# Runs of small TensorE instructions in the planned order of a two-layer decoder trunk

## The chip, the core and the metric

The kernel runs on one core of a Trainium2 chip. A core has five engines that work at the same time, each through its own queue in order: TensorE (matrix products; PE in the profile, its weight loads PEld), VectorE (DVE), ScalarE (ACT), GpSimd (POOL) and SyncE (SP, which here issues all DMA transfers). An engine waits at an instruction until its semaphores say that the inputs are there. The metric is the time of one execution in device microseconds (us). It is the median of several runs.

## The reference, cut to what matters

The program computes a trunk of two layers over 256 tokens of width 1024, in float32. Each layer is one attention part and one feed-forward part, both between normalisations:

```python
for l in range(DEPTH):                                   # 2
    h = _rms_norm(x, g_pre_mix[l])
    parts = jnp.split(h @ w_in[l], split_at, axis=-1)    # 1024 x 2840: q, six k/v sets, gates, fox q/k/v, forget
    o_nsa = _nsa_mixer(...)     # 8 heads, 2 kv groups: compressed + selected + window attention, gated
    o_fox = _fox_mixer(...)     # 8 heads of causal attention with a forget bias
    mix = jnp.concatenate([o_nsa, o_fox], axis=-1) @ w_out[l]
    x = x + _rms_norm(mix, g_post_mix[l])
    h = _rms_norm(x, g_pre_mlp[l])
    y = jnp.square(jax.nn.relu(h @ w_up[l])) @ w_down[l]  # 1024 x 4096, 4096 x 1024
    x = x + _rms_norm(y, g_post_mlp[l])
return x
```

At this length all four key blocks are among the selected ones, so the selected branch is plain causal attention, and so is the window branch.

## The kernel before, in words

**The work.** Tokens stand in two halves of 128. A weight matrix arrives in pieces of up to 512 KB (`wraw`). ScalarE rounds each piece to a high part `whi`, VectorE subtracts to get the low part `wlo`, and TensorE takes three rounded products instead of one exact one (`mm3`, line 683): activation high by weight high, activation high by weight low, activation low by weight high. These *weight products* are 2,592 of TensorE's instructions, most of them 512 columns wide.

**The other instructions.** TensorE has 609 more products, which read no `whi` or `wlo`. The text calls them small. In the attention part of each layer they are:

- transposes in full float32 against the identity in `cst`, whose output goes to a PSUM tile `s`: probabilities `pr` in threes (`probs_T`, line 1279), keys, q and others in fours. The text calls these T.
- scores of the NSA heads, `s<-kx,qS` and `x<-kx,qS` (`nsa_scores`, line 1234): rounded and 128 by 128, like the weight products.
- fox scores `s<-fkT,fqT` (`fox_scores`, line 1223): groups that use 64 rows of the array. The text calls them K.
- products of probabilities with values, `o<-prT,vS` and the like (`pv`, line 1298): groups that use 64 columns. The text calls them V.
- products in 32 columns for the compression network (`o<-w,kstk`), and rounded transposes against `identr`.

**The order.** Nobody writes the order of instructions by hand. The program first records every operation with its inputs (`Recorder.add`, line 206), a sequence number (`key`) and an estimated cost (`_cost`, line 466). Then `Recorder.schedule` (line 316) plays the five engines through time. Whenever an engine is free, it takes the ready operation with the lowest rank whose tiles fit in the buffers that are free. For TensorE the rank is the key; for the other engines it is a due time, which `deadlines` (line 260) works back from TensorE's planned times. `order` (line 288) repeats this for five passes and two starting ranks and for each of five stages (bounds in `stages`), and keeps the ranks whose planned end was earliest. `emit` (line 417) writes the operations out in that order; line 424 issues every one of them, so almost every row of the profile has L424. A `stretch` is a group of products that the planner keeps together as one operation: the three transposes of one `pr`, one group of fox scores, one group of values.

In its plan the planner charges TensorE 90 ns when it goes from the full array to a group in part of it and 200 ns when it leaves such a group for any other shape (`ENTER`, `LEAVE`, line 44). It charges nothing between weight products and full-array transposes.

**Buffers.** PSUM has eight banks: three for tag `s`, two each for `x` and `acc`, one for `o` (`psum`, line 550). Raw weights have nine buffers, `whi` and `wlo` seven each (line 50). SyncE issues DMAs in the planned order, each when its buffer is free.

**The start.** The first 512 columns of the input projection come in eight transfers (`first`), then weight pieces, x (four transfers) and constants alternate on SyncE's queue. While TensorE multiplies the second chunk (288 columns wide, in four pieces of 12 products each), ScalarE takes the squares of x (`squares_of_x`, line 709; rows `rl<-x`) and VectorE the factor `rsqrt`, which the two small products of `row_scales` (line 1169) spread over the columns.

Of the kernel before, what the change touches and what calls it, by code (L numbers as in the profile page):

```python
# [45 lines left out]
EVKEY = 1  # L46
FIRSTS = [(k, k + 1) for k in range(8)]
NFIRST = 768
UPK = 7
TOK, WBUFS, RBUFS = 6, 7, 9  # L50
LOAD_LEAD, SPLIT_LEAD = 12, 1
# [125 lines left out]


class Op:
    __slots__ = ("engine", "name", "args", "kw", "key", "urgent", "cost", "deps", "succs", "bufs",  # L180
                 "missing", "ready", "start", "end", "tile", "rank")


class Recorder:
# [21 lines left out]
    def add(self, engine, name, args, kw):  # L206
        if self.group is not None:
            assert engine == "tensor"
            self.group.append((name, args, kw))
            return  # L210
        op = Op()
        op.engine, op.name, op.args, op.kw = engine, name, args, kw
        op.key = len(self.ops) if self.key is None else self.key
        if self.lane is not None and self.key is None:
            op.key = self.lane + LANE * (len(self.ops) - self.lane)
        op.urgent = self.hot
        views = []
        for _, a, k in args[2] if name == "stretch" else [(name, args, kw)]:
            views += [(i == 0, v) for i, v in enumerate(a) if isinstance(v, View)]
            views += [(i in ("out", "accum_out"), v) for i, v in k.items() if isinstance(v, View)]  # L220
        op.tile = _tile(op) if engine == "tensor" else None
        op.cost = _cost(op, views) + SLACK.get(engine, 0)
        deps = {} if self.after is None else {self.after: -1e9}
        op.bufs = []
        for is_out, v in sorted(views, key=lambda x: x[0]):
            b, m = v.buf, v.mask()
            if b not in op.bufs:
                op.bufs.append(b)

            def against(entries):  # L230
                for o, p, q, bank in entries:
                    if o is not op and o not in deps and (
                            (bank and engine == "tensor") or
                            (p[0] < v.p[1] and v.p[0] < p[1] and (m & q).any())):
                        deps[o] = _latency(o, op)

            against(b.writes)
            entry = (op, v.p, m, is_out and b.psum and engine == "tensor")
            if is_out:
                against(b.reads)  # L240
                b.writes = [w for w in b.writes if not (
                    w[0] in deps and v.p[0] <= w[1][0] and w[1][1] <= v.p[1] and not (w[2] & ~m).any())]
                b.writes.append(entry)
            else:
                if b.psum:
                    for o, _, _, _ in b.reads:
                        if o.engine != engine and o is not op and o not in deps:
                            deps[o] = 130.0
                b.reads.append(entry)
        op.deps = deps  # L250
        for b in op.bufs:
            if not b.ops:
                self.fifo.setdefault(b.tag, []).append(b)
            b.ops += 1
        op.succs = []
        for d in deps:
            d.succs.append(op)
        self.ops.append(op)
# [57 lines left out]
    def schedule(self):  # L316
# [35 lines left out]
                    taken[b.tag] = n + 1  # L352
            return True

        force = False
        events = [(0.0, 0, None)]
        count, out, live = 0, [], set()
        while events:
            t, _, released = heapq.heappop(events)
            if released is not None:  # L360
                free[released] += 1
            if events and events[0][0] == t:
                continue
            for e, ops in waiting.items():
                while busy[e] <= t:
                    best = None
                    for op in ops:
                        if op.ready <= t and (best is None or (best.urgent, -best.rank) < (op.urgent, -op.rank)) and fits(op):
                            best = op
                    if best is None:  # L370
                        break
                    if not best.urgent and e != "tensor" and not force:
                        q = hot[e]
                        while q and q[0].start is not None:
                            q.popleft()
                        memo = {}
                        if any(estimate(op, memo) < t + WAIT * best.cost for op in list(q)[:4] if op.start is None and fits(op)):
                            break
                    ops.remove(best)
                    for b in best.bufs:  # L380
                        if b not in live:
                            live.add(b)
                            free[b.tag] -= 1
                            head[b.tag] += 1
                    best.start = t
                    out.append(best)
                    if e == "sync":
                        busy[e] = t + 450
                        bus = max(bus, t + 1150) + best.cost + RAMP.get(loads, 0)
                        best.end = bus + 900 + (LATE if loads >= len(FIRSTS) else 0)  # L390
                        loads += 1
                    else:
                        busy[e] = best.end = t + best.cost
                        if e == "tensor" and best.tile != tiled:
                            busy[e] = best.end = best.end + (tiled == (P, P)) * ENTER + (tiled != (P, P)) * LEAVE
                            tiled = best.tile
                    count += 1
                    heapq.heappush(events, (busy[e], count, None))
                    for b in best.bufs:
                        left[b] -= 1  # L400
                        if not left[b]:
                            count += 1
                            heapq.heappush(events, (best.end + (260 if b.psum else 150), count, b.tag))
                    for s in best.succs:
                        s.ready = max(s.ready, t, best.end + s.deps[best])
                        s.missing -= 1
                        if not s.missing:
                            waiting[s.engine].append(s)
                            count += 1
                            heapq.heappush(events, (s.ready, count, None))  # L410
            force = not events and len(out) < len(self.ops)
            if force:
                heapq.heappush(events, (t + 100, 0, None))
# [22 lines left out]
def _tile(op):  # L436

    up = lambda n: next(m for m in (32, 64, P) if n <= m)
    lhsT = op.args[1]
    return (P, P) if op.name == "transpose" else (up(lhsT.shape[0]), up(int(np.prod(lhsT.shape[1:]))))  # L440
# [25 lines left out]
def _cost(op, views):  # L466

    out = op.args[0] if op.args else op.kw["out"]
    n = int(np.prod(out.shape[1:]))
    part = 100 * (out.shape[0] < P)  # L470
    if op.engine == "gpsimd":
        return 200 + 0.72 * n + 10 * int(np.prod(out.shape[1:-1]))
    if op.engine == "sync":
        v = views[0][1]
        return v.shape[0] * int(np.prod(v.shape[1:])) * 4 / 360.0
    if op.engine == "tensor":
        if op.name == "stretch":
            side = P // min(op.tile)
            return sum(_product(*x[:2], side) for x in op.args[2][::side])
        return _product(op.name, op.args, 1)  # L480
    if op.engine == "vector":
        if op.name == "reciprocal":
            return 60 + 6.5 * n
        if op.name == "tensor_reduce":
            n = int(np.prod(op.args[1].shape[1:]))
        fast = op.name in ("tensor_copy", "tensor_scalar", "memset") and not any(v.buf.psum for _, v in views)
        aps = sum(isinstance(v, View) for v in op.args[2:4]) if op.name == "tensor_scalar" else int(
            op.name == "scalar_tensor_tensor" and isinstance(op.args[2], View))
        return 68 + part + 64 * aps + n * (0.52 if fast else 1.04) + 10 * (op.name == "tensor_tensor_reduce")
    src = op.args[1]  # L490
    aps = sum(isinstance(op.kw.get(k), View) for k in ("bias", "scale", "accum_out"))
    return n / 1.2 + (55 if src.buf.psum else 92) + 93 * aps
# [1139 lines left out]
```

## Time and profile before

| | before |
|---|---|
| time, median of 3 runs | 620.45 us (620.43 to 620.82) |
| the profiled execution | 620.69 us, of which the span is 618.4 us |
| TensorE busy | 611.2 us, 99% of the span |
| its weight loads | 511.7 us, 83% |
| VectorE, ScalarE busy | 467.0 us (76%), 391.6 us (63%) |
| chain that ended last | TensorE 99% |

A row of a group says: line, engine, operation, output<-inputs, shape, count, busy us, mean ns of one, and the idle time before it. In a row of the timeline the first number is the start in us and the second the length from there to the end of the last instruction merged into it. Products overlap, each beginning while the one before still runs, so the price of a product is read from start to start of neighbouring rows and not from its length.

The layers show as stretches: attention of the first layer to about 125 us, its feed-forward part to about 310 us, attention of the second layer to about 430 us, its feed-forward part to the end.

### The profile page before, as it was taken

To read this page: it belongs to the slowest core of one execution; us is meant where nothing else is said; L and a number is where in the kernel's file an instruction comes from. 1 tells how busy PE (TensorE), PEld (TensorE's weight loads), DVE (VectorE), ACT (ScalarE), POOL (GpSimd) and SP (SyncE) were. 2 spreads that over 40 slices of the span, in tenths; PEclk is the share of its full clock that TensorE was granted. 3 is DMA by queue.
4 is the path that set the end of the run, shared out by engine and by line. 5 is a ranking of instruction groups with operands and counts; after the bars stand their busy time and mean duration, and the time that the engine had idled before them with its cause. 6 is when DMAs were issued, how large, how long until landed. Compare 5 with 4: busy or idle time off the path is not lost.

```text
span 618.4 us, 9735 instructions
## 1 busy us (share of the span) xinstructions
PE 611.2 (99%) x3430; PEld 511.7 (83%) x3430; DVE 467.0 (76%) x1029; ACT 391.6 (63%) x768; POOL 9.2 (1%) x20
## 2 busy tenths in 40 slices
PE   9999999999999999999999999999999999999995
PEld 7988887788888888888888888777888888888884
DVE  7799998789966567556598899896996575566544
ACT  6767978567655556555466768775776456556522
POOL 0000100000000000000000021000000000000000
PEclk9999999999999999999999999999999999999999
DMA  8987547518755565554346782553386555555001
GB/s 321 400 323 259 204 143 256 181 40 316 239 196 190 180 203 194 190 193 138 109 153 228 256 306 83 202 206 103 131 284 218 187 201 174 201 194 183 33 1 68
DMA packets 34817, 118.86 MB, mean 192 GB/s; under 512 B 4144, under 2 KB 4304, under 8 KB 34768
## 3 DMA queue, kind: packets, MB, share of 16 engines
q1 hardware_dynamic: 34768, 118.23, 55.8%
q8 instruction: 27, 0.44, 0.3%
q14 instruction: 22, 0.18, 0.1%
HBM read 117.15 MB, written 1.07 MB: 191 GB/s over the span
## 4 chain that ended last, share of the span: by engine, by line
PE 99%; DVE 0%; DVEq 0%; issue 0%; ACT 0%
PE s L424 35%; PE acc L424 31%; PE x L424 25%; PE o L424 7%; DVE x L424 0%; DVE m L424 0%; DVEq L1628 0%; DVE rsqrt L424 0%; ACT rl L424 0%
## 5 line engine op out<-in xcount | busy, mean ns | idle before, releaser
L424 DVE TENSOR_TENSOR wlo<-wraw,whi 128x1024 fp32r<-128x1024 f32 (+1 forms) x188 | 225.2, 1200 | 98.0 <-ACT whi L424 58.1
L424 ACT ACTIVATE whi<-wraw 128x1024 fp32r<-128x1024 f32 (+1 forms) x188 | 195.0, 1041 | 100.9 <-PE acc L424 68.5
L424 PE MATMUL s<-xT,whi 128*128 128x512 f32 x448 | 106.5, 390 | 0.0
L424 PEld LDWEIGHTS s<-xT,whi 128*128 128x128 f32 x448 | 83.3, 188 | 16.8
L424 PE MATMUL x<-whi,aT 128*128 128x512 f32 x256 | 88.6, 390 | 0.0
L424 PE MATMUL acc<-whi,aT 128*128 128x512 f32 x256 | 88.3, 389 | 0.0
L424 PEld LDWEIGHTS s<-xT,wlo 128*128 128x128 f32 x448 | 57.4, 191 | 2.2
L424 PE MATMUL s<-xT,wlo 128*128 128x256 f32 x448 | 58.1, 283 | 0.0
L424 PEld LDWEIGHTS acc<-whi,aT 128*128 128x128 f32 x256 | 48.0, 188 | 10.0
L424 PEld LDWEIGHTS x<-whi,aT 128*128 128x128 f32 x256 | 48.1, 188 | 9.5
L424 PE MATMUL x<-wlo,aT 128*128 128x512 f32 x128 | 50.0, 390 | 0.0
L424 PE MATMUL acc<-wlo,aT 128*128 128x512 f32 x128 | 49.9, 390 | 0.0
L424 ACT ACTIVATE pr<-pr,st 128x256 f32<-128x256 f32 (+1 forms) x96 | 42.8, 449 | 7.2 <-DVE st L424 6.7
L424 PE MATMUL acc<-whi,xT 128*128 128x512 f32 (+1 forms) x128 | 37.4, 354 | 0.0
L424 PE MATMUL acc<-xT,whi 128*128 128x512 f32 x128 | 36.1, 402 | 0.0
L424 PE MATMUL x<-whi,xT 128*128 128x512 f32 x112 | 35.8, 399 | 0.0
L424 ACT ACTIVATE h<-s 128x256 f32<-128x256 f32 x56 | 21.2, 378 | 16.0 <-PE s L424 16.0
L424 ACT ACTIVATE rl<-h 128x512 f32<-128x512 f32 x28 | 17.7, 633 | 18.1 <-DVE h L424 18.1
L424 PEld LDWEIGHTS acc<-wlo,aT 128*128 128x128 f32 x128 | 24.0, 188 | 5.0
L424 ACT ACTIVATE rl<-x 128x512 f32<-128x512 f32 x24 | 14.6, 610 | 21.0 <-PE x L424 16.9
L424 PEld LDWEIGHTS x<-wlo,aT 128*128 128x128 f32 x128 | 24.1, 188 | 4.5
L424 PEld LDWEIGHTS acc<-xT,whi 128*128 128x128 f32 x128 | 22.7, 188 | 5.3 <-ACT whi L424 0.8
(218 smaller groups left out, 966.0 us busy)
## 6 DMA issues: line engine op xcount, KB each, us to landing
wraw<-in_w_up_dram SPq DMA_DIRECT2D x64, 512.0 KB, 4.0
wraw<-in_w_down_dram SPq DMA_DIRECT2D x64, 512.0 KB, 4.2
wraw<-in_w_in_dram SPq DMA_DIRECT2D x36, 512.0 KB, 4.3
wraw<-in_w_out_dram SPq DMA_DIRECT2D x16, 512.0 KB, 6.7
w<-in_cmp_w_k_dram SPq DMA_DIRECT2D x8, 512.0 KB, 5.4
w<-in_cmp_w_v_dram SPq DMA_DIRECT2D x8, 512.0 KB, 5.6
bias<-sums SPq DMA_DIRECT2D x8, 384.0 KB, 6.9
first<-in_first_dram SPq DMA_DIRECT2D x7, 384.0 KB, 6.2
```

Source lines behind the costliest of these rows:

```text
L424: getattr(getattr(self.nc, op.engine), name)(*[real(v) for v in args], **{k: real(v) for k, v in kw.items()})
```

## The change

`schedule` now knows which of TensorE's operations are small: those that read no `whi` or `wlo` tile. Two rules act at the moment when TensorE is free and the lowest-ranked ready operation has been found. Neither acts on operations marked urgent.

- If that operation is small, the last one taken was not, and it has been ready for less than `HOLD` = 300 ns, the planner counts the small operations that are ready and fit. If there are fewer than two, it takes the lowest-ranked weight product instead, if one is ready.
- If the last one taken was small and the best is a weight product, the planner takes a small one instead, when one is ready whose rank is at most `REACH` = 40 above the weight product's.

```diff
+HOLD = 300
+REACH = 40
...
+        op.small = engine == "tensor" and not any(v.buf.name.startswith(("whi", "wlo")) for _, v in views)
...
-        force = False
+        force = small_last = False
...
                     if best is None:
                         break
+                    if e == "tensor" and best.small and not small_last and not best.urgent and t < best.ready + HOLD:
+                        more = [op for op in ops if op.ready <= t and fits(op)]
+                        if sum(op.small for op in more) < 2:
+                            best = min((op for op in more if not op.small), key=lambda op: op.rank, default=best)
+                    if e == "tensor" and small_last and not best.urgent and not best.small:
+                        more = [op for op in ops if op.small and op.ready <= t and op.rank < best.rank + REACH and fits(op)]
+                        best = min(more, key=lambda op: op.rank, default=best)
...
                         busy[e] = best.end = t + best.cost
+                        small_last = best.small if e == "tensor" else small_last
```

The number of instructions stays the same on every engine. In TensorE's order the unbroken runs of small instructions go from 135 to 82; the shortest that vanish are single NSA score products that stood between weight products. How the kinds follow one another in TensorE's order, counted in the two programs (T, K and V as above; R is any rounded full-array product, weight products and NSA scores alike):

| kind followed by kind | before | after |
|---|---|---|
| V by R, V by T | 6, 2 | 2, 6 |
| K by R, K by T, K by V | 4, 3, 1 | 4, 2, 2 |
| R by V, T by V | 6, 1 | 5, 1 |
| R by K, T by K | 8, 0 | 6, 2 |
| blocks of T entered | 82 | 78 |

Because the due times of the other engines are worked back from TensorE's plan, their orders change too. At the start SyncE's order after `first` goes from wraw, wraw, x, wraw, x, wraw, x, x, wraw, cst to wraw, x, x, wraw, x, x, cst, wraw, wraw, wraw, and ScalarE takes the first squares of x right after the split of the first piece, where it first took two splits.

More of the change, by code (lines that the diff above doesn't have):

```diff
@@ L179 @@
 class Op:
-    __slots__ = ("engine", "name", "args", "kw", "key", "urgent", "cost", "deps", "succs", "bufs",
+    __slots__ = ("small", "engine", "name", "args", "kw", "key", "urgent", "cost", "deps", "succs", "bufs",
                  "missing", "ready", "start", "end", "tile", "rank")
```

## The prediction

> **What bounds the kernel now.** I read the page first, then the busy time by stretch, then what TensorE's loads wait for, then the timeline.
>
> ```profile
> span 618.4 us, 9735 instructions
> PE 611.2 (99%) x3430; PEld 511.7 (83%) x3430; DVE 467.0 (76%) x1029; ACT 391.6 (63%) x768; POOL 9.2 (1%) x20
> PEclk9999999999999999999999999999999999999999
> PE 99%; DVE 0%; DVEq 0%; issue 0%; ACT 0%
> ```
>
> TensorE is busy for 611.2 of 618.4 us at full granted clock, and 99% of the chain that ended last lies on it. A busy PE could still hide waits, so the stretches and the waits come next: attention of the first layer (60 to 125 us), a feed-forward stretch, and the loads' waits in the first of these.
>
> ```profile
> 60.00:125.00 65.00, 65.00 (x420) 51.67 (x419) 57.81 (x210) 49.37 (x146) 3.39 (x8) 1.00 0.58 198
> 160.00:300.00 140.00, 140.00 (x709) 119.64 (x708) 90.24 (x109) 77.61 (x104) 0.00 (x0) 1.00 0.57 187
> ```
>
> ```profile
> PEld s L424 <- ACT pr L424: 0.9, 3, 0.3
> PEld s L424 <- DVE pr L424: 0.4, 1, 0.4
> PEld s L424 <- ACT prT L424: 0.4, 1, 0.4
> ```
>
> The second and third numbers of a stretch are its length and PE's busy time: no gap in either. Loads waited for an input 5 times in this stretch, 1.7 us together, and a load runs ahead of its product, so the products lost less than that. The change can therefore take only what switching between kinds of products costs, and it can add waits that are not there now.
>
> **What a switch costs.** Prices are read from start to start.
>
> ```profile
> 99.25 0.39 PE L424 MATMUL acc<-wlo,oT 128*128 128x512 f32 x1
> 99.48 0.40 PE L424 MATMUL acc<-whi,oT 128*128 128x512 f32 x1
> 99.72 0.49 PE L424 MATMUL s<-cst,pr 128*128 128x128 f32 x3
> 99.96 0.48 PE L424 MATMUL acc<-whi,oT 128*128 128x512 f32 x1
> 100.37 0.93 PE L424 MATMUL s<-fkT,fqT 64*128 64x128 f32 x8
> 101.23 0.51 PE L424 MATMUL acc<-wlo,oT 128*128 128x512 f32 x1
> 101.66 0.87 PE L424 MATMUL o<-prT,vS 128*64 128x256 f32 x8
> ...
> 104.42 0.87 PE L424 MATMUL s<-cst,pr 128*128 128x128 f32 x6
> 105.05 0.48 PE L424 MATMUL acc<-whi,oT 128*128 128x512 f32 x1
> 105.36 0.40 PE L424 MATMUL x<-whi,oT 128*128 128x512 f32 x1
> 105.59 0.40 PE L424 MATMUL x<-wlo,oT 128*128 128x512 f32 x1
> ```
>
> A weight product after another takes 0.23 (99.25 to 99.48). Three T take 0.24 (99.72 to 99.96) and make the next product 0.08 longer (105.05 to 105.36 is 0.31): 0.32 for three, 0.107 each. That is what a T costs anyway, since six T in one run take 0.63 + 0.08 = 0.71 after a V, which itself makes the first one longer. So joining two runs of T saves 0.00 to 0.02.
>
> K costs 0.10 on entry (99.96 to 100.37 is 0.41, against 0.31 for a product after T) and 0.11 on exit to a product. After K and before V one product takes 0.43 (101.23 to 101.66): 0.23, that 0.11, and 0.09 for the entry to V. An exit from V to T costs 0.71 less six T at 0.109, 0.055.
>
> ```profile
> 412.62 0.93 PE L424 MATMUL s<-fkT,fqT 64*128 64x128 f32 x8
> 413.47 1.52 PE L424 MATMUL o<-prT,fV 128*64 128x256 f32 x16
> 414.92 0.50 PE L424 MATMUL acc<-whi,oT 128*128 128x512 f32 x1
> 415.26 0.40 PE L424 MATMUL acc<-wlo,oT 128*128 128x512 f32 x1
> ```
>
> Here K goes straight to V. K takes 0.85, as it did at 100.37 (0.86), and V to R costs 0.34 - 0.23 = 0.11. So K next to V pays neither exit nor entry, 0.20 less than with a product between.
>
> The Trainium skill ("TensorEngine Tiling (Array Packing)", Key Properties) says that changing the tiling mode drains TensorE. The 0.09 to 0.11 above agree. By that rule alone changes of mode would be what counts, and the table of the change has 31 for K and V before and 30 after: one less, 0.1 to 0.2 us. The 0.055 for an exit to T is beyond it.
>
> ```profile
> 91.94 0.39 PE L424 MATMUL s<-kx,qS 128*128 128x256 f32 x2
> 92.17 0.63 PE L424 MATMUL x<-kx,qS 128*128 128x512 f32 x2
> 92.63 0.40 PE L424 MATMUL x<-whi,oT 128*128 128x512 f32 x1
> 92.87 0.39 PE L424 MATMUL x<-wlo,oT 128*128 128x512 f32 x1
> ```
>
> NSA scores cost 0.23 for two of 256 columns, 0.23 for one of 512, and 0.24 for the weight product behind them: they are as cheap among weight products as these among themselves. More than half of the 53 vanished runs are scores of this kind alone, and their vanishing is worth nothing in these rows.
>
> **The sum.** (1) Exits from V: before 6 x 0.11 + 2 x 0.055 = 0.77, after 2 x 0.11 + 6 x 0.055 = 0.55, so -0.22. (2) Exits from K: 4 x 0.11 + 3 x 0.055 = 0.605, after 4 x 0.11 + 2 x 0.055 = 0.55, so -0.055. (3) Entries to V from outside K or T: 6 to 5, -0.09. Entries to K from T (none before, two after) are unseen; between 0 and the 0.10 from a product I take 0.10, since V after T pays too, and 0 would give 0.2 more. (4) Blocks of T: 82 to 78 at 0.00 to 0.02, -0.05. Together -0.4.
>
> (5) Weight products near small ones are a little longer. The numbers below are the shortest, the median and the longest.
>
> ```profile
> L424 PE MATMUL x<-whi,oT x64: 387/396/484, 92.6 to 428.0; 128*128 128x512 f32 x64
> L424 PE MATMUL x<-whi,aT x256: 389/389/481, 148.3 to 606.2; 128*128 128x512 f32 x128
> ```
>
> The median is 7 ns above that of the feed-forward stretch. Over some 300 products (my estimate: two or three behind each of the 135 runs) this is 2 us. If it belongs to the runs, 40% fewer of them give back 0.8; if it belongs to the stretch, nothing. I take 0.3, nearer to nothing, because more than half of the vanished runs are such scores.
>
> (6) Waits. I cost them at nothing, and name the cover. A small instruction held back costs none while a weight product is ready, and in this stretch TensorE has no gap. One pulled forward is taken only when the plan has it ready. What would be late next is the copying of a finished `s` bank:
>
> ```profile
> L424 ACT ACTIVATE prT<-s 128x384 f32<-128x384 f32 x32 | 15.0, 483 | 3.2 <-PE s L424 3.1
> ```
>
> 0.48 us for a bank that three T fill in 0.33. With three banks the third group of a run is covered, a fourth is not. Bounds: the 1.7 us above and, supposed, as much in the second layer could vanish from the loads (at most -3, since some of it is hidden), or every mixed run could wait (below). I keep 0.
>
> (7) The start, where the orders of SyncE and ScalarE change. The third weight piece of the second chunk moves behind x and the constants.
>
> ```profile
> 7.80 0.33 SPq L424 DMA_DIRECT2D wraw<-in_w_in_dram  x1
> ...
> 12.41 0.33 SPq L424 DMA_DIRECT2D wraw<-in_w_in_dram  x1
> ```
>
> ```profile
> wraw<-in_w_in_dram SPq DMA_DIRECT2D x8, 288.0 KB, 5.0
> ```
>
> ```profile
> 16.44 0.42 PE L424 MATMUL acc<-whi,xT 128*128 128x288 f32 x2
> ...
> 22.13 0.39 PE L424 MATMUL s<-cst,rsqrt 128*128 128x128 f32 x2
> ```
>
> ```profile
> 14.66 0.69 ACT L424 ACTIVATE whi<-wraw 128x576 fp32r<-128x576 f32 x1
> ```
>
> ```profile
> 15.38 0.76 DVE L424 TENSOR_TENSOR wlo<-wraw,whi 128x576 fp32r<-128x576 f32 x1 [0.22 <-ACT whi L424]
> ```
>
> It goes out at 12.41 at the latest (before at 7.80) and lands 5.0 later, by 17.4. The chunk's products run 0.132 apart (43 from 16.44 to 22.13), so the third piece is wanted at 16.44 + 24 x 0.132 = 19.6. The split on ScalarE takes about 0.7, the subtraction 0.76: ready near 19.0 even if both start at the landing. It is hidden with 0.6 to spare; without that cover it costs what it is late, up to 0.5.
>
> Sum: -0.4 - 0.3 = -0.7 us. Against the profiled execution of 620.69 (span 618.4 and 2.3 around it) that is 620.0; the median of the runs is 0.24 below that execution, so 620.45 - 0.7 = **619.7 us**. From no change a measurement of this kernel can tell about 0.2%, 1.24 us: the forecast is a gain too small for that.
>
> **The rivals.** *Every run has a price of its own.* If entering and leaving any run, scores too, costs 0.03, which start times in hundredths can't exclude, 53 fewer give 1.6, with (1) to (3) 2.0: 618.4. For it speak the 7 ns, against it the 0.24 at 92.63. *Longer runs fill the `s` banks faster than they are emptied* (the other side). Some 20 runs now write two or more `s` banks in a row. Each bank takes 0.48 to copy and 0.33 to fill, so a run whose banks are still held waits 0.15 and the signal, say 0.2: 20 x 0.2 - 0.7 = +3.3, 623.7. It decides against the change by 0.2% from a mean of 0.1 per run ((1.24 + 0.7) / 20). For it: the bank waits on ScalarE in the loads' list. Against it: they were 0.4 at the longest, and between these runs lie more weight products than before. *The change does nothing on the chip*: the plan differs, (1) to (4) are given back by one or two new waits like those of 0.4 listed: 620.5. *By the drain rule*, one change of mode less: 620.45 - 0.2 = 620.2; the exits to T at 0.055 speak against it.
>
> **How the numbers follow.** Forecast 46%, price per run 28%, banks 16%, nothing 7%, drain rule 3%. The price per run crosses the 1.24 at 0.016 a run, so nearly all of its chance is faster by over 0.2%, and a part of the forecast's spread with (5) at its end of 0.8 reaches it too: 0.30. Banks give slower: 0.16. The rest is 0.54 for no difference. The forecast's own range is 619.1 (0.8 at step 5) to 620.4. The whole range goes down to 618.2, past the rival of 618.4 by its rounding, and up to 621.9, into the lower part of the banks; beyond lie most of that rival and a tail below, under 2 in 10.
>
> **What would show it.** V groups followed by T at 0.055; the stretch from 60 to 125 shorter by 0.3 to 0.5; medians of x<-whi,oT nearer to 389; PE still without a gap. New waits of loads for ACT prT or DVE kinds, summing to over 2 us, would make it wrong on one side; a stretch shorter by over 0.8 on the other. A hole in TensorE near 20 us would show the start wrong.

## The result and the profile after

The change makes the kernel a little faster. Its median is 619.36 us (618.98 to 619.79, 16 runs) against 620.66 us for the kernel before (16 runs): a ratio of 0.9979, with a 95% interval of 0.9972 to 0.9986, so 0.9 to 1.7 us. A second comparison (the first experiment) gives 619.58 against 620.61: 0.9985, interval 0.9976 to 0.9994. Both intervals leave out 1, so there is a gain. That it passes the 0.2% that the prediction set as the bound is not shown.

The same lines of the page as before, now of the changed kernel:

```profile
span 617.7 us, 9715 instructions
PE 610.5 (99%) x3430; PEld 512.0 (83%) x3430; DVE 465.9 (75%) x1029; ACT 392.4 (64%) x768; POOL 8.7 (1%) x20
PEclk9999999999999999999999999999999999999998
PE 99%; DVE 0%; issue 0%; DVEq 0%; ACT 0%
```

TensorE still bounds the kernel over its whole length. Its busy time and the span are both 0.7 us shorter. The profiled execution took 619.79 us, the longest of the 16 and 0.43 above their median. The stretches show where a part of that comes from:

```profile
60.00:125.00 65.00, 64.88 (x419) 51.79 (x419) 56.27 (x205) 49.96 (x145) 4.42 (x8) 1.00 0.55 197
160.00:300.00 140.00, 140.00 (x708) 119.66 (x707) 89.81 (x109) 77.71 (x104) 0.00 (x0) 1.00 0.57 186
```

PE was busy for 64.88 of the 65.00 us of the first stretch, where it had no gap before. The timeline of TensorE has the place, first in this execution, then in the profiled execution of the same program in the first experiment:

```profile
65.78 1.11 PE L435 MATMUL acc<-xT,wlo 128*128 128x256 f32 x8
67.01 0.34 PE L435 MATMUL s<-identr,pcs 128*128 128x128 f32 x2
```

```profile
65.84 1.12 PE L435 MATMUL acc<-xT,wlo 128*128 128x256 f32 x8
66.79 0.29 PE L435 MATMUL s<-identr,pcs 128*128 128x128 f32 x2
```

Eight weight products and the step to the transposes of `pcs` take 1.23 us in the one and 0.95 in the other. So the one execution waited 0.28 us there, and the other did not. The loads' waits in the same stretch of the changed kernel are

```profile
PEld s L435 <- ACT pr L435: 0.6, 2, 0.3
PEld s L435 <- ACT prT L435: 0.4, 1, 0.4
PEld s L435 <- ACT prX L435: 0.4, 1, 0.4
```

1.4 us in four waits, after 1.7 in five: the same size, and no single wait is longer.

Where the time was saved can be read from one group, the high-part products of the feed-forward down projection, whose first and last start stand in the row. First the changed kernel, then its second profile (the row of before stands in the prediction: 148.3 to 606.2):

```profile
L435 PE MATMUL x<-whi,aT x256: 389/389/481, 148.0 to 605.5; 128*128 128x512 f32 x128
```

```profile
L435 PE MATMUL x<-whi,aT x256: 389/389/481, 147.7 to 605.3; 128*128 128x512 f32 x128
```

The first layer's attention and input projection give 0.3 us in the profile with the wait and 0.6 without it. The distance from first to last, in which the second layer's attention lies, goes from 457.9 to 457.5 and 457.6: another 0.3 to 0.4.

**The prices of the switches, in the changed kernel's timeline:**

```profile
99.59 0.39 PE L435 MATMUL acc<-wlo,oT 128*128 128x512 f32 x1
99.91 0.93 PE L435 MATMUL s<-fkT,fqT 64*128 64x128 f32 x8
100.77 0.87 PE L435 MATMUL o<-prT,vS 128*64 128x256 f32 x8
...
102.77 0.82 PE L435 MATMUL o<-prX,vW 128*64 128x256 f32 x8
103.52 0.87 PE L435 MATMUL s<-cst,pr 128*128 128x128 f32 x6
104.15 0.70 PE L435 MATMUL acc<-whi,oT 128*128 128x512 f32 x2
104.69 0.40 PE L435 MATMUL acc<-wlo,oT 128*128 128x512 f32 x1
...
108.12 0.49 PE L435 MATMUL s<-cst,pr 128*128 128x128 f32 x3
108.54 0.93 PE L435 MATMUL s<-fkT,fqT 64*128 64x128 f32 x8
```

K goes straight to V at 99.91 and takes 0.86, as in the profile before. Behind a V, six T take 0.63 (103.52 to 104.15), and the two products behind them 0.54, 0.08 more than two at 0.23: 0.71 in all, the same as in the profile before. T straight to K, which the profile before did not have, takes 0.42 for three T (108.12 to 108.54), 0.09 more than their 0.33.

**The start.** SyncE's queue and TensorE in the changed kernel, then the same product in the kernel before:

```profile
10.58 0.33 SPq L435 DMA_DIRECT2D cst<-in_consts_dram  x1
11.55 2.05 SPq L435 DMA_DIRECT2D wraw<-in_w_in_dram  x3
```

```profile
16.46 0.42 PE L435 MATMUL acc<-whi,xT 128*128 128x288 f32 x2
...
24.18 0.40 PE L435 MATMUL x<-wlo,xT 128*128 128x512 f32 x1
```

```profile
24.18 0.40 PE L424 MATMUL x<-wlo,xT 128*128 128x512 f32 x1
```

The third piece goes out at 11.55, behind x and the constants. The chunk still starts at 16.4 to 16.5 us, and the fifth product of the next chunk at 24.18 in both kernels. The moved transfers show no cost here.

### The profile page after: what moved, and what is told of

Its sections match the earlier page's. It is cut to its first block, busy times and chain, and to the rows that moved or that the text cites. A ratio compares the mean times of both kernels' runs of the same rounds, so it can differ in the third digit from the quotient of the medians.

```text
span 617.7 us, 9715 instructions
## 1 busy us (share of the span) xinstructions
PE 610.5 (99%) x3430; PEld 512.0 (83%) x3430; DVE 465.9 (75%) x1029; ACT 392.4 (64%) x768; POOL 8.7 (1%) x20
## 4 chain that ended last, share of the span: by engine, by line
PE 99%; DVE 0%; issue 0%; DVEq 0%; ACT 0%
PE s L435 35%; PE acc L435 31%; PE x L435 25%; PE o L435 7%; DVE x L435 0%; DVE m L435 0%; DVEq L1639 0%; DVE rsqrt L435 0%; ACT rl L435 0%
## 5 line engine op out<-in xcount | busy, mean ns | idle before, releaser
L435 PE MATMUL acc<-whi,xT 128*128 128x512 f32 (+1 forms) x128 | 34.5, 348 | 0.0
L435 PE MATMUL acc<-xT,whi 128*128 128x512 f32 x128 | 33.9, 398 | 0.0
```

The costliest lines, as they stand in the source:

```text
L435: getattr(getattr(self.nc, op.engine), name)(*[real(v) for v in args], **{k: real(v) for k, v in kw.items()})
```

## The experiments

Two theories stood against each other. Theory A is the prediction's: only the switches between kinds of products count, and waits where they come. Theory B is its first rival: each run of small instructions has a price of its own. A third, that any new plan moves the time by this much, is tested by one run. Differences are of medians, against runs of the kernel before on the same chip.

**The change again.**

> The changed kernel once more, beside the others. Theory A (the price of switching between kinds of products: exits from the 64-row and 64-column groups, blocks of transposes): -0.4 us plus a small remainder, about -0.7. Theory B (every run of small instructions has a price of its own of 0.02 to 0.03): 53 runs fewer and the kinds, -1.5 to -2.0. Theory C (it is the new plan of the other engines, not TensorE's own order): no number of its own, whatever the first measurement gave, -1.3.

Measured: 619.58, -1.03 us (ratio 0.9985, 0.9976 to 0.9994). The gain repeats.

**A longer reach.**

```diff
-REACH = 40
+REACH = 400
```

> REACH 400 in place of 40, with the holding back taken out is not meant: only the reach is changed. Runs fall to 87 as in the changed kernel, but exits, entries and blocks of transposes come out at the same total price as before the change (5.13 against 5.14 us). Theory A: no difference from before, -0.3 to +0.3. Theory B: 48 runs fewer at 0.02 to 0.03, -1.0 to -1.4. A loss of over 0.5 would be waits.

Measured: 620.20, -0.41 us (0.9995, 0.9986 to 1.0003). It has 87 runs, almost as few as the change, but its switches, priced as in the prediction, cost what they cost before. Theory B wanted 48 runs x 0.03 = 1.4 us, or 1.0 at 0.02 a run; the interval ends at 0.9. The -0.41 is a little beyond theory A's -0.3 too; the table below says where it lies.

**Runs taken apart.** Neither rule; after a small instruction the planner prefers a weight product to a small one that is ready.

```diff
+                    if e == "tensor" and small_last and not best.urgent and best.small and t < best.ready + 1000:
+                        more = [op for op in ops if not op.small and op.ready <= t and fits(op)]
+                        best = min(more, key=lambda op: op.rank, default=best)
```

> The opposite rule: after a small instruction a ready weight product is taken first. 215 runs instead of 135, 119 blocks of transposes instead of 82, 44 blocks of rounded transposes instead of 11. Theory A by the prices from the trace: +2.2 us. Theory B: 80 runs more at 0.02 to 0.03 on top, +3.8 to +4.6. Waits can add to either and would show as loads waiting for ACT or DVE.

Measured: 622.12, +1.51 us (1.0025, 1.0015 to 1.0035), with 215 runs. Below both theories, and nearer to A.

**Another plan without either rule.** One pass of the planner less.

```diff
-PASSES = 4
+PASSES = 3
```

> The kernel before with one planning pass fewer: the rule on TensorE is not there, but all engines get another plan (132 runs, all prices as before). Theories A and B: no difference, -0.2 to +0.2. Theory C: a difference of the size of the change's, 0.5 to 1.5 to either side.

Measured: 620.77, +0.16 us (1.0003, 0.9994 to 1.0012). This one other order of the other engines, with TensorE's switches as before, gives nothing that stands out of the noise. It is one plan of many, and some of the plans below do bring waits.

**Each rule alone.** First only the holding back (the second rule's three lines left out), then only the taking on (the first rule's four lines left out).

> Only the holding back, without the taking on. 116 runs instead of 135, the switches between kinds at nearly the price of before (5.10 against 5.14 us). Theory A (prices of the switches, and 0.007 us for each run, which is what the first runs leave): -0.2. Theory B (0.03 for each run): -0.6.

Measured: 620.19, -0.50 us (0.9992, 0.9983 to 1.0000). By its median that is nearer to theory B's -0.6 than to theory A's -0.2; the interval, 0 to -1.1, holds both, so this run does not decide.

> Only the taking on, without the holding back. 88 runs, switches at 4.89 instead of 5.14 us. Theory A: -0.25 for the switches and 47 x 0.007 for the runs, -0.6. Theory B: -0.25 and 47 x 0.03, -1.7.

Measured: 620.20, -0.49 us (0.9993, 0.9984 to 1.0002). With 88 runs left theory B wanted 1.7, and the interval ends at 1.0. The two halves add up to the gain of the whole, within their intervals.

**Taking on only behind a group in part of the array.**

```diff
-                    if e == "tensor" and small_last and not best.urgent and not best.small:
+                    if e == "tensor" and small_last and not best.urgent and not best.small and tiled != (P, P):
```

(and without the first rule)

> The taking on only while the array stands in a part shape, so that only what follows a 64-row or 64-column group can change. 132 runs. Four exits from 64-column groups go to transposes instead of two, but the one direct step from a 64-row to a 64-column group is lost and two more entries are paid: by the prices 5.24 against 5.14 us. Theory A: +0.1. A rule of thumb that any joining helps: -0.1 or better.

Measured: 620.79, +0.10 us (1.0001, 0.9992 to 1.0009). Here the new plan made as many dear switches as it removed, and the time stayed.

**Holding back for longer.**

```diff
-HOLD = 300
+HOLD = 600
```

> HOLD 600 in place of 300, REACH as in the changed kernel. 77 runs, switches at 4.63, a little cheaper than in the changed kernel. Theory A without waits: -0.9, as the changed kernel. But an operation held for 600 ns is late for what depends on it: the weight products that need the transposed, normalised activations. If that bites, waits of 1 to 3 us appear on TensorE around 44, 130 and 317 us (the turned queries and the transposes of mg), and the time is +0.5 to +2 against before.

Measured: 622.74, +2.05 us (1.0036, 1.0022 to 1.0049). TensorE's waits and its timeline:

```profile
PE s L435 <- DVE q_rot L435: 1.0, 1, 1.0
PE s L435 <- ACT xT L435: 0.2, 1, 0.2
```

```profile
43.48 0.46 PE L435 MATMUL s<-identr,q_rot 128*128 128x128 f32 x4
44.91 1.19 PE L435 MATMUL s<-identr,q_rot 128*128 128x128 f32 x12 [0.97 <-DVE q_rot L435]
...
129.73 1.42 PE L435 MATMUL s<-cst,mg 128*128 128x128 f32 x8
131.36 0.50 PE L435 MATMUL s<-whi,xT 128*128 128x512 f32 x1 [0.21 <-ACT xT L435]
131.69 0.40 PE L435 MATMUL s<-wlo,xT 128*128 128x512 f32 x1
132.20 0.73 PE L435 MATMUL s<-whi,xT 128*128 128x512 f32 x2
```

The same transposes of `mg` in the change, with `HOLD` 300:

```profile
128.02 0.60 PE L435 MATMUL s<-cst,mg 128*128 128x128 f32 x4
128.37 0.48 PE L435 MATMUL acc<-whi,oT 128*128 128x512 f32 x1
128.69 0.60 PE L435 MATMUL s<-cst,mg 128*128 128x128 f32 x4
129.05 0.48 PE L435 MATMUL acc<-whi,oT 128*128 128x512 f32 x1
```

With `HOLD` 600, sixteen transposes of `q_rot` come in one run, and the fifth waits for VectorE. The eight transposes of `mg`, which the change lays in two groups of four with a weight product between (0.35 us from a group's start to that product), come in one run too. They take 1.63 us to the next product in place of 0.7, and that product and those behind it wait for the copies of their outputs. This is akin to the prediction's rival of the `s` banks, a run that gets ahead of the engines that feed and empty it, but at the inputs and at the stage's end rather than in the `s` banks of the probabilities.

**Transposes alone taken apart.** As the third experiment, with `small` true only for products with `cst`.

```diff
+        op.small = engine == "tensor" and any(v.buf.name == "cst" for _, v in views)
```

> Neither rule; instead, full float32 transposes alone are kept apart: after a T the planner takes a weight product if one is ready. Blocks of T go from 82 to 124, runs from 135 to 163; entries and exits of K and V stay nearly as before. Theory A (kinds that follow one another, a block of T at 0.00 to 0.02): 0.0 to +0.8, I take +0.4. Theory B (each run has a price of its own of about 0.03, or products stay longer behind each): +0.8 to +1.3.

Measured: 621.63, +1.02 us (1.0015, 1.0007 to 1.0024). By its total that is theory B. The waits say otherwise:

```profile
PE acc L431 <- DVE fqT L431: 0.7, 1, 0.7
```

```profile
47.54 0.58 PE L431 MATMUL x<-kx,qS 128*128 128x512 f32 x1
47.96 0.38 PE L431 MATMUL s<-cst,lf 128*128 128x128 f32 x2
48.10 0.48 PE L431 MATMUL x<-kx,qS 128*128 128x512 f32 x1
49.27 0.50 PE L431 MATMUL acc<-xT,whi 128*128 128x512 f32 x1 [0.69 <-DVE fqT L431]
```

From 48.10 to 49.27 are 1.17 us in place of about 0.31, so one late copy of `fqT` on VectorE makes 0.86 of the 1.0. The 42 further blocks of T are left with little. The new plan also has two steps from K straight to V where there was one, three exits from V to T where there were two, and one entry to V fewer, which at the prediction's prices is about -0.25; the expectation took these as nearly unchanged.

**Scores alone gathered.** Both rules, with `small` true only for products with `kx` or `vbig`.

```diff
+        op.small = engine == "tensor" and any(v.buf.name in ("kx", "vbig") for _, v in views)
```

> Both rules, but only NSA scores and the product of pc and values count as small. Runs go from 135 to 110, those of scores alone from 35 to 12; blocks of T 82 to 83. The new plan also moves some entries and exits: K followed by V 1 to 2, V by T 2 to 3, R by K 8 to 5 and T by K 0 to 3. Theory A: the vanished score runs are worth nothing, only the moved entries and exits count: -0.2. Theory B (a price for every run, scores too): 25 x 0.03, -0.8, and the -0.2: -1.0.

Measured: 620.55, -0.06 us (1.0000, 0.9991 to 1.0009). The runs fall from 135 to 110, those of scores alone from 35 to 12, and the time stays. Theory B's -1.0 lies outside the interval, which ends at -0.6.

**A little more holding back.** `HOLD` 400.

> The changed kernel with HOLD 300 raised to 400: 81 runs, 75 blocks of T, two fewer exits of K to T. Between the change (no lasting wait) and 600 (waits at 44 and at 131 us). Theory A: as the change, -0.9 to -1.2, if no hole comes; if the waits at 44 and 131 us begin here, +0.5 or more.

Measured: 620.26, -0.35 us (0.9996, 0.9987 to 1.0005): most of the gain is gone, though it has 81 runs and 75 blocks of T. Its largest wait:

```profile
32.78 0.84 PE L435 MATMUL x<-whi,xT 128*128 128x512 f32 x3
33.90 0.50 PE L435 MATMUL x<-wlo,xT 128*128 128x512 f32 x1 [0.28 <-DVE wlo L435]
```

Three products take 1.12 us in place of 0.68: a subtraction on VectorE is late in the new plan.

**All of them side by side.** I took TensorE's start times in each profile, from the fourth weight product to the last product. Waits are steps from start to start that are more than 0.04 us above the usual one between the same kinds. What is left without them I compare with before, which had no such wait. Each row is one profiled execution, so waits and rest need not add up to the difference of the medians.

| kernel | runs | blocks of T | time, us | waits, us | rest, us |
|---|---|---|---|---|---|
| the change, first profile | 82 | 78 | -1.30 | 0.28 | -0.84 |
| the change, second profile | 82 | 78 | -1.03 | 0.00 | -0.99 |
| reach 400 | 87 | 82 | -0.41 | 0.10 | -0.31 |
| all apart | 215 | 119 | +1.51 | 0.57 | +1.17 |
| one pass less | 132 | 82 | +0.16 | 0.34 | +0.21 |
| holding back only | 116 | 83 | -0.50 | 0.52 | -0.32 |
| taking on only | 88 | 78 | -0.49 | 0.42 | -0.49 |
| only behind part of the array | 132 | 82 | +0.10 | 0.00 | -0.02 |
| hold 600 | 77 | 74 | +2.05 | 2.90 | -0.70 |
| T apart | 163 | 124 | +1.02 | 0.96 | -0.20 |
| scores only | 110 | 83 | -0.06 | 0.29 | -0.38 |
| hold 400 | 81 | 75 | -0.35 | 1.30 | -1.03 |

The rest does not go by the number of runs: 87 runs give -0.31 and 88 give -0.49 where 82 give -0.84 to -0.99, and 163 give -0.20. A part of it goes by neither runs nor switches. The starts of the rounded products of 512 columns (weight products and NSA scores) that stand between rounded products, counted as their time beyond 227 ns each, give 0.4 us less in both profiles of the change, 0.15 to 0.35 less in every other plan with one or both rules, and 0.25 and 0.3 less in the two plans that take runs apart, with 163 and 215 runs; with one pass less it is 0.05. Without this part the rest is about 0.0 for reach 400, 0.0 for holding back only and -0.2 for taking on only. The prices of the switches gave 0.0, 0.0 and -0.25 for these three. So the prices fit these three, and the common part is something else, whose cause these runs do not show. With one pass less they do not fit: 0.26 is left where they gave nothing. The waits differ from plan to plan by up to 1.3 us without any of the mechanisms that the change aims at, and 2.9 at hold 600. The change is faster than all the others because its rest is among the lowest and its plan has almost no wait. No variant beat it.

## Why the prediction was right

The forecast was 0.7 us less, 619.7; two comparisons measured 1.3 and 1.0 less, 619.4 and 619.6. The direction was right, and the profiles find the gain at the two places that it named; their sum was undersized by 0.3 to 0.6 us. For the second place the reason that it gave did not hold.

**Steps 1 to 4, the switches (forecast -0.4).** Their prices held where the changed kernel shows them: exit from V to T by six T in 0.71, K next to V at no further price, and T into K at 0.09 where the prediction took 0.10 unseen. The starts of TensorE's products beside another kind give about -0.6 in both profiles of the change. Of this -0.4 is the listed counts at the listed prices; the remaining 0.2 is spread over places that I did not take apart. Step 4 took a block of T at 0.00 to 0.02. With 42 more blocks the rest was -0.20; of that the 512-column products make about -0.25 and the moved switches of K and V about -0.25, so 0.3 is left, 0.007 a block.

**Step 5, longer weight products (forecast -0.3, between 0 and -0.8).** These are the rows of the changed kernel, and below them the second group's row of the kernel before:

```profile
L435 PE MATMUL x<-whi,oT x64: 387/393/504, 92.9 to 426.9; 128*128 128x512 f32 x64
L435 PE MATMUL acc<-whi,oT x64: 388/389/499, 95.9 to 433.2; 128*128 128x512 f32 x64
```

```profile
L424 PE MATMUL acc<-whi,oT x64: 389/393/504, 93.3 to 433.9; 128*128 128x512 f32 x64
```

The medians fall from 396 to 393 and from 393 to 389 ns, 389 being that of the feed-forward stretch. Over all rounded 512-column products that stand between rounded ones, the starts give -0.41 and -0.39, of which the weight products alone are -0.28. That is the size of the forecast, but not for its reason. The prediction's condition was that the time belongs to the runs, so that fewer runs give it back. It fell by 0.25 and 0.3 also in the kernels with 163 and 215 runs, where there were 135 before. So it does not go by their number, and that the size came out near 0.3 was luck. What it hangs on stays open.

**Step 6, waits at nothing.** Right for this plan, with one wait of 0.28 us in one of two profiles. It was the step on which most depended: hold 400 lost 1.3 us to waits with nearly the same runs and switches, in places that the prediction's list of loads' waits did not hold (`wlo`, the copies of `xT`).

**Step 7, the start.** Right: the third piece goes out at 11.55, before the latest time assumed, and TensorE shows no hole near 20 us.

**The stretch from 60 to 125 us** was to be shorter by 0.3 to 0.5. A window of fixed length can't show this; up to 148 us the first layer gained 0.3 with the wait and 0.6 without.

**The rivals.** *A price for every run* falls by reach 400, by taking on alone and by scores alone, which all removed 25 to 48 runs for less than it asked. It asked for -2.0 in all, and -1.0 to -1.3 came. The intervals of these three leave out 0.02 a run; against a smaller price speaks the kernel with 80 runs more, which came out below what theory A's switches alone were to cost (+1.51 against +2.2). *Banks* did not come at `HOLD` 300; a wait of this family comes at 600, and there it costs more than the whole gain. *Nothing* falls by both intervals. *The drain rule*: the profile after again shows 0.055 for an exit to T, beside 0.11 to a weight product, and the gain of 1.0 to 1.3 is beyond the 0.2 of one change of mode less. The Trainium skill ("TensorEngine Tiling (Array Packing)", Key Properties) says that a change of tiling mode drains TensorE. The 0.11 for an exit to a weight product agrees; K straight to V is such a change too, and showed no further price. In these profiles the neighbours set how much a change costs.

## What to carry to other kernels

Where one engine is busy throughout, price an order by the pairs of neighbours that it contains, each read from start to start, and not by the number of groups: runs of the same kind of work as its surroundings cost nothing to break. A rule in a planner re-times all the other engines as well, and the waits that come and go with each new plan (0 to 1.3 us here) can be larger than what the rule gains; take them out, from the starts of the bound engine, before judging the rule by its total. And one profile may carry a wait that the next does not have, so look at two before placing a difference of a few tenths.

## What was not expected

- Blocks of full float32 transposes cost almost nothing to split: 42 more of them left the time without waits 0.2 us below that of before, and 0.3 above what the other changes of that plan would give.
- Holding small instructions back 100 ns longer changed runs and switches hardly at all (82 to 81 runs), and brought 1.3 us of waits at 33, 130 and 315 us in its profile.
- The rounded 512-column products came a little closer together in every plan with a changed rule, with more runs as with fewer.
- The two rules add, within their intervals: -0.50 and -0.49 us alone, -1.03 and -1.30 together.
